# A decoder layer in split float32: first rounding on two engines, squares behind the up weights, a split bias product, and the last head's scores later

## The chip, the cores and the metric

One core of a Trainium2 chip. The metric is the device time of one execution in microseconds. The engines are named PE (TensorE), ACT (ScalarE), DVE (VectorE), POOL (GpSimd) and SP (SyncE, which here issues loads).

## The reference

The kernel computes one decoder layer for 256 tokens of width 1024, in float32: a half step of a SwiGLU feed-forward net, a mixer of two groups of attention heads that share a table of relative position biases, cross attention to 256 memory tokens in 4 heads of width 256, a second half step, and a final norm. Cut to what matters here:

```python
def rms_norm(x, g):
    xf = x.astype(jnp.float32)
    y = xf * lax.rsqrt(jnp.mean(xf * xf, axis=-1, keepdims=True) + NORM_EPS)
    return (y * g.astype(jnp.float32)).astype(x.dtype)

def swiglu(x, w_gu, w_down):
    gu = x @ w_gu
    g, u = jnp.split(gu, 2, axis=-1)
    return (jax.nn.silu(g) * u) @ w_down

def reference(x, mem, ...):
    x = x + 0.5 * swiglu(rms_norm(x, g_ffn1), w_ffn1_gu, w_ffn1_down)
    h = rms_norm(x, g_mix)           # q, k, v of both groups
    ...                              # s = q @ k.T * scale + rel_bias[bucket of the distance]
    x = x + concat([ya, yb]) @ w_out
    # cross attention, per head
    #   s = q @ k.T * 256 ** -0.5; p = softmax(s); o = p @ v
    x = x + o @ w_co
    x = x + 0.5 * swiglu(rms_norm(x, g_ffn2), w_ffn2_gu, w_ffn2_down)
    return rms_norm(x, g_final)
```

## The kernel before, in words

PE multiplies in a rounded 32-bit type, fp32r. To keep float32 accuracy an operand is split in a high part (rounded by a copy on ACT) and a low part (the difference, on DVE): `wsplit` (L124) does it for a weight chunk of 128x1024, with the copy at L125 and the difference at L126; `split` does it for activations (L320 and L321, or with a gain as scale L323 and L324). A product of two split operands is `mm3`, three products (L188 high by high, L189 low of the first by high, L190 high by low of the second), or `mm2`: one of 512 columns over the high and low part of the activations (L224, and L238 in the first stage where both halves are 256 wide), and one of 256 columns with the low part of the weight (L228).

Weights come from device memory in chunks through SP's queue (L118) into a few `raw` buffers and are split into a pool of `w` buffers, each of which is used again when PE has read it for the last time.

The order of the work on PE is the order in which the code issues it, helped by a small event list: `later(us, f, ...)` calls `f` when a clock has moved on by that many modelled microseconds; every product moves the clock by its modelled length (`tick`). The order on the other engines is set by a scheduler, except in `start`, which is in a manual schedule for all engines.

The pieces that the change touches:

- `start` (L754): loads the input x in pieces (`x0`), warms PE with WARM and then WARM - 1 products of the identity (L770, L796), turns x with transposes (L779), and computes the first gate chunk `pg0` over k = 0 to 7 with `mmT_wide` (L238), while `prepare` brings the next two k: the weight's split, copies of the turned x to X (L783), and their split with the gain (L323, L324). `token_squares` sums the squares of x (L337, ACT with accumulation): half at k = 2, half at k = 5 behind the split of the first "up" weights, where the sum is added (L806). From it come the mean, a power on POOL (L330), a diagonal on DVE (L376) and products that spread it over the rows (L382).
- `bias_table` and `bias_rows` (L88, L96): load the logarithm table `lnt`, the one-hot table `oht` of 32x383 and `rel_bias` as `rbt` (L93); 4 modelled us later multiply `rbt` and `oht` in full float32 (L98), add, and send the rows through device memory on POOL's queue. On SP's queue the load of `rbt` stands right behind the loads of the gains (L72) of `start`, and those of `lnt` (L91) and `oht` (L92) among later weight loads.
- `cross_qp` (L678): projects the query, splits it, and for head h sets off `scores(h)` after a delay: three products each (L188 to L190) for the halves, the maximum (L693), the exponential on ACT (L698), the division (L701); and `turn(h)` 5 modelled us after the scores, which transposes the probabilities (L709) and splits them (L320, L321).
- `cross_o(h)` (L729): waits until `PT[h]`, the turned probabilities, has been issued, and multiplies them with the values (L188 to L190); its output is split as well. The call of `addT(w_co, OT, ...)` that follows multiplies the outputs of the heads with `w_co`; `cross_o` of heads 2 and 3 is called between its blocks.

Of the kernel before, what the change touches and what calls it, by code (L numbers as in the profile page):

```python
# [9 lines left out]
F32 = mybir.dt.float32  # L10
F32R = mybir.dt.float32r
BF = mybir.dt.bfloat16
AF = mybir.ActivationFunctionType
OP = mybir.AluOpType
# [8 lines left out]
NB = 383  # L23
# [5 lines left out]
def layer_kernel(ctx, tc, x_in, mem_in, g_ffn1, w_gu1, w_dn1, g_mix, w_in, rel_bias, g_out_a, g_out_b,  # L29
# [57 lines left out]

    def bias_table():  # L88
        lnt = work.tile([16, NB], F32, tag="g1", name="lnt", bufs=3)
        oht = work.tile([32, NB], F32, tag="g1", name="oht", bufs=3)  # L90
        nc.sync.dma_start(lnt, lnc)  # L91
        nc.sync.dma_start(oht, onehot)  # L92
        nc.sync.dma_start(rbt, rel_bias)  # L93
        later(4.0, bias_rows, lnt, oht)

    def bias_rows(lnt, oht):  # L96
        ps = bank()
        nc.tensor.matmul(ps[:16, :NB], rbt, oht, start=True, stop=True)  # L98
        rb = work.tile([16, 384], F32, tag="u1", name="rb")
        nc.vector.tensor_add(rb[:, :NB], ps[:16, :NB], lnt)  # L100
        nc.vector.memset(rb[:, NB:], 0.0)
        scr = dram.tile([16, 32, 384], F32, name="scr")
        nc.gpsimd.dma_start(scr, rb.unsqueeze(1).broadcast_to([16, 32, 384]))
        for i in range(2):
            f = const.tile([P, 8, 256], F32, tag="big", name="F", bufs=2)
            for a in range(4):
                src = bass.AP(tensor=scr.tensor, offset=scr.offset + 127 - 32 * a + i * 8 * 32 * 384,
                              ap=[[383, 32], [32 * 384, 8], [1, 256]])
                later(5.0 * (i * 4 + a), nc.gpsimd.dma_start, f[32 * a:32 * a + 32], src)
            F.append(f)  # L110
# [12 lines left out]

    def wsplit(w, raw, a, b):  # L124
        nc.scalar.activation(w[:, 0, a:b], raw[:, a:b], AF.Copy)  # L125
        nc.vector.tensor_tensor(w[:, 1, a:b], raw[:, a:b], w[:, 0, a:b].bitcast(F32), OP.subtract)  # L126

    def cols(wd, k0, nk, c0, n):
# [29 lines left out]
    def later(delay, fn, *args):  # L158
        events.append((clock[0] + delay, len(events_seq), fn, args))
        events_seq.append(0)  # L160
        events.sort(key=lambda e: e[:2])
# [171 lines left out]
    def token_squares(src, ss):  # L333

        for tb in range(2):
            junk = work.tile([P, 512], BF, tag="sq", name="junk", bufs=3)
            nc.scalar.activation(junk, src[:, tb * 512:tb * 512 + 512], AF.Square, accum_out=ss[:, tb:tb + 1])  # L337
# [340 lines left out]
    def cross_qp(xs, K, st):  # L678
# [37 lines left out]
        for c in range(2):  # L716
            for blk, ps in enumerate(projT(colchunk(w_cq, c * 512, 512), xs, 4, spread=(c == 0), whole=4 * (c == 0))):
                if blk % 2 == 0:
                    Q.append(slot())
                if ps.shape[-1] == 512:  # L720
                    t = work.tile([P, 256], F32, tag="sq", name="hq", bufs=3)
                    halves(t, ps)
                    ps = t
                split(Q[-1], blk % 2, 1, ps)
                if blk % 2:
                    later(3.0 + 3.0 * (blk // 2) * (c == 0), scores, c * 2 + blk // 2)
        return PT

    def cross_o(V, PT, OT, h):  # L729
# [24 lines left out]
    def start():  # L754
# [18 lines left out]
        def prepare(j):  # L773
            banks = [bank(), bank()] if j == 0 else [bank()] * 2
            xp = [banks[i][:, i * 256:i * 256 + 256] for i in range(2)]
            for i in range(2):
                for tb in range(2):
                    o = tb * 512 + ((j * 2 + i) % 4) * P
                    nc.tensor.transpose(xp[i][:, tb * P:(tb + 1) * P], x0[j // 2][:, o:o + P], ident)  # L779
            if j > 0:  # L780
                wsplit(ws[j], raws[j], 0, 1024)
                for i in range(2):
                    nc.scalar.activation(X[j * 2 + i], xp[i], AF.Copy)  # L783
            for i in range(2):
                split(xs[j], i, 1, X[j * 2 + i] if j else xp[i], gain("ffn1", j * 2 + i))
                if j == 0:
                    wsplit(ws[j], raws[j], i * 512, i * 512 + 512)
            if j == 0:
                for i in range(2):
                    nc.scalar.activation(X[i], xp[i], AF.Copy)  # L790
# [1 line left out]
        xss = [small.tile([P, 2], F32, tag=f"xss{hf}", name="xss", bufs=1) for hf in range(2)]  # L792

        prepare(0)
        for i in range(WARM - 1):
            nc.tensor.matmul(gps[:, :P], ident, ident, start=True, stop=True)  # L796
        for k in range(KT):
            mmT_wide(pg0, first, xs, k, k == 0, k == KT - 1)
            if k % 2 == 0 and k < KT - 2:
                prepare(k // 2 + 1)  # L800
                if k == 2:
                    token_squares(x0[0], xss[0])
            if k == 5:
                up.extend(colchunk(w_gu1, FF, 512))
                token_squares(x0[1], xss[1])
                nc.vector.tensor_tensor(xss[0], xss[0], xss[1], OP.add)  # L806
                st.given(xss[0], 7.0)
                later(4.0, turn_gains)
# [162 lines left out]
```

## Time and profile before

| | us |
|---|---|
| median of three runs | 606.03 |
| the runs | 605.70, 606.03, 606.17 |
| the profiled execution | 605.48 |
| its span, first to last instruction | 603.7 |
| PE busy | 595.4 (99% of the span) |
| DVE busy | 435.5 (72%) |
| ACT busy | 348.2 (58%) |
| POOL busy | 51.9 (9%) |

The profiled execution's time is its span and 1.8 us around it. The granted clock of PE was 0.998 of full speed over the span. A product's record covers its way through the array, and records overlap, so what a product costs PE is read from start to start. In a timeline row the first number is the start, the second the length from the start of the first to the end of the last of the instructions that the row joins; in brackets stands how long the engine was idle before, and what ended that.

### The profile page before, as it was taken

To read this page: it belongs to the slowest core of one execution; us is meant where nothing else is said; L and a number is where in the kernel's file an instruction comes from. 1 tells how busy PE (TensorE), PEld (TensorE's weight loads), DVE (VectorE), ACT (ScalarE), POOL (GpSimd) and SP (SyncE) were. 2 spreads that over 40 slices of the span, in tenths; PEclk is the share of its full clock that TensorE was granted. 3 is DMA by queue.
4 is the path that set the end of the run, shared out by engine and by line. 5 is a ranking of instruction groups with operands and counts; after the bars stand their busy time and mean duration, and the time that the engine had idled before them with its cause. 6 is when DMAs were issued, how large, how long until landed. Compare 5 with 4: busy or idle time off the path is not lost.

```text
span 603.7 us, 9507 instructions
## 1 busy us (share of the span) xinstructions
PE 595.4 (99%) x3528; PEld 519.9 (86%) x3528; DVE 435.5 (72%) x730; ACT 348.2 (58%) x606; POOL 51.9 (9%) x83
## 2 busy tenths in 40 slices
PE   9999999999999999999999999999999999999995
PEld 8988888888899888888888899888888888888885
DVE  4878756897565876766897787869878787784424
ACT  6856445655545677656675565657754655653303
POOL 0000210000010102103300120003100000000000
PEclk9999999999999999999999999999999999999999
DMA  7866998577577636444446544444565566476401
GB/s 238 286 209 224 214 245 248 181 241 242 174 232 221 210 107 209 140 140 140 141 126 214 186 154 159 141 139 132 160 220 191 171 209 209 154 265 197 153 0 71
DMA packets 58990, 110.04 MB, mean 182 GB/s; under 512 B 3760, under 2 KB 14608, under 8 KB 58944
## 3 DMA queue, kind: packets, MB, share of 16 engines
q1 hardware_dynamic: 57664, 105.49, 54.7%
q0 software_dynamic: 832, 2.88, 2.7%
q10 hardware_dynamic: 448, 1.05, 0.5%
q8 instruction: 28, 0.46, 0.3%
q14 instruction: 18, 0.15, 0.1%
HBM read 107.58 MB, written 1.84 MB: 181 GB/s over the span
## 4 chain that ended last, share of the span: by engine, by line
PE 92%; DVE 3%; ACT 1%; issue 1%; DMA 1%; POOL 0%; POOLq 0%; ACTq 0%; SPq 0%
PE bank L224 42%; PE bank L228 21%; PE bank L188 7%; PE bank L189 7%; PE bank L190 7%; PE bank L238 3%; DVE w L126 1%; PE bank L518 1%; PE bank L575 1%; PE bank L558 1%; DMA raw<-in_w_co_dram 1%; DVE slot L321 1%; ACT w L125 1%; ACT cpt L698 0%; PE bank L770 0%
## 5 line engine op out<-in xcount | busy, mean ns | idle before, releaser
L224 PE MATMUL bank<-slot,w 128*128 128x512 f32 x1130 | 353.7, 396 | 0.0
L126 DVE TENSOR_TENSOR w<-raw,w 128x1024 fp32r<-128x1024 f32 (+1 forms) x197 | 237.1, 1217 | 82.5 <-ACT w L125 81.7
L125 ACT ACTIVATE w<-raw 128x1024 fp32r<-128x1024 f32 (+1 forms) x197 | 202.5, 1051 | 87.3 <-PE bank L190 43.4
L228 PEld LDWEIGHTS bank<-slot,w 128*128 128x128 f32 x1130 | 209.7, 188 | 48.6 <-issue 1.0
L228 PE MATMUL bank<-slot,w 128*128 128x256 f32 x1130 | 222.5, 279 | 0.0
L224 PEld LDWEIGHTS bank<-slot,w 128*128 128x128 f32 x1130 | 174.0, 189 | 2.5 <-issue 0.6
L188 PE MATMUL bank<-w,slot 128*128 128x512 f32 (+1 forms) x156 | 60.6, 389 | 0.0
L190 PE MATMUL bank<-w,slot 128*128 128x512 f32 (+1 forms) x156 | 60.0, 384 | 0.0
L189 PE MATMUL bank<-w,slot 128*128 128x512 f32 (+1 forms) x156 | 59.9, 384 | 0.0
L277 ACT ACTIVATE hv<-bank 128x256 f32<-128x256 f32 x108 | 39.7, 374 | 34.9 <-PE bank L228 34.4
L190 PEld LDWEIGHTS bank<-w,slot 128*128 128x128 f32 x156 | 29.3, 188 | 6.0
L188 PEld LDWEIGHTS bank<-w,slot 128*128 128x128 f32 x156 | 29.3, 188 | 5.8 <-issue 0.3
L189 PEld LDWEIGHTS bank<-w,slot 128*128 128x128 f32 x156 | 29.3, 188 | 5.5
L320 ACT ACTIVATE slot<-u 128x512 fp32r<-128x512 f32 x22 | 13.8, 629 | 33.7 <-DVE u L434 33.7
L238 PE MATMUL bank<-slot,w 128*128 128x256 f32 x240 | 31.8, 289 | 0.0
L238 PEld LDWEIGHTS bank<-slot,w 128*128 128x128 f32 x240 | 30.0, 194 | 0.5 <-DVE slot L324 0.4
L355 POOL TENSOR_TENSOR ssq<-ssq,sq 128x256 f32<-128x256 f32 x22 | 20.6, 935 | 78.5 <-ACT sq L350 78.3
L429 ACT ACTIVATE g<-g 128x512 f32<-128x512 f32 x22 | 13.8, 631 | 20.6 <-DVE g L292 20.6
L324 DVE SCALAR_TENSOR_TENSOR slot<-X,gT,slot 128x256 fp32r<-128x256 f32 x30 | 19.4, 658 | 6.9 <-ACT slot L323 6.9
L278 DVE TENSOR_TENSOR u<-bank,hv 128x256 f32<-128x256 f32 x40 | 16.7, 418 | 8.8 <-ACT hv L277 8.7
L278 DVE TENSOR_TENSOR g<-bank,hv 128x256 f32<-128x256 f32 x40 | 16.3, 417 | 8.3 <-ACT hv L277 8.3
L323 ACT ACTIVATE slot<-X,gT 128x256 fp32r<-128x256 f32 x30 | 14.8, 505 | 13.0 <-DVE X L303 12.9
(129 smaller groups left out, 494.0 us busy)
## 6 DMA issues: line engine op xcount, KB each, us to landing
raw<-in_w_ffn_gu_dram SPq DMA_DIRECT2D x88, 512.0 KB, 4.8
raw<-in_w_ffn_down_dram SPq DMA_DIRECT2D x44, 512.0 KB, 4.5
raw<-in_w_ckv_dram SPq DMA_DIRECT2D x16, 512.0 KB, 5.3
raw<-in_w_in_dram SPq DMA_DIRECT2D x12, 512.0 KB, 3.6
raw<-in_w_in_dram SPq DMA_DIRECT2D x24, 256.0 KB, 4.1
raw<-in_w_out_dram SPq DMA_DIRECT2D x8, 512.0 KB, 4.4
raw<-in_w_cq_dram SPq DMA_DIRECT2D x8, 512.0 KB, 5.8
raw<-in_w_co_dram SPq DMA_DIRECT2D x8, 512.0 KB, 4.0
```

What stands on the lines that cost most here:

```text
L125: nc.scalar.activation(w[:, 0, a:b], raw[:, a:b], AF.Copy)
L126: nc.vector.tensor_tensor(w[:, 1, a:b], raw[:, a:b], w[:, 0, a:b].bitcast(F32), OP.subtract)
L188: nc.tensor.matmul(ps, ah, bh, start=start, stop=False)
L189: nc.tensor.matmul(ps, al, bh, start=False, stop=False)
L190: nc.tensor.matmul(ps, ah, bl, start=False, stop=stop)
L224: nc.tensor.matmul(ps, w[:, 0, o + blk * P:o + (blk + 1) * P], both(xs, k), start=k == first, stop=False)
L228: nc.tensor.matmul(ps[:, :256], w[:, 1, o + blk * P:o + (blk + 1) * P], both(xs, k)[:, :256], start=False, stop=k == last)
L238: nc.tensor.matmul(ps, w[:, wp_, o + blk * P:o + (blk + 1) * P], a, start=start and i == 0, stop=stop and i == 2)
L277: nc.scalar.activation(t, ps[:, 256:], AF.Copy)
L278: nc.vector.tensor_tensor(out, ps[:, :256], t, OP.add)
L324: nc.vector.scalar_tensor_tensor(l, src, g, h.bitcast(F32), OP.mult, OP.subtract)
L355: (eng or nc.gpsimd).tensor_tensor(new, self.ss, sq, OP.add)
```

## The change

Four edits. In `start` the first half of the first weight is rounded by ACT and DVE, 256 columns each (`wsplit2`), and one product of the identity is left out behind `prepare(0)`. All four squares of x are issued at k = 5, behind the up weights. In `bias_table` the one-hot table gets a 384th column of zeros, `rbt` is split into `rbs` (ACT, DVE), the one-hot table is copied to fp32r (`ohr`, ACT), and `bias_rows` makes two fp32r products of 384 columns. In `cross_qp` the delay of the last head's scores is 5.7 instead of 3.0 modelled us (the others keep 3, 6 and 3).

```diff
@@ -87,15 +87,22 @@
 
     def bias_table():
         lnt = work.tile([16, NB], F32, tag="g1", name="lnt", bufs=3)
-        oht = work.tile([32, NB], F32, tag="g1", name="oht", bufs=3)
+        oht = work.tile([32, 384], F32, tag="g1", name="oht", bufs=3)
+        nc.vector.memset(oht[:, NB:], 0.0)
         nc.sync.dma_start(lnt, lnc)
-        nc.sync.dma_start(oht, onehot)
+        nc.sync.dma_start(oht[:, :NB], onehot)
         nc.sync.dma_start(rbt, rel_bias)
-        later(4.0, bias_rows, lnt, oht)
-
-    def bias_rows(lnt, oht):
+        rbs = small.tile([32, 2, 16], F32R, tag="rbs", name="rbs", bufs=1)
+        nc.scalar.activation(rbs[:, 0], rbt, AF.Copy)
+        nc.vector.tensor_tensor(rbs[:, 1], rbt, rbs[:, 0].bitcast(F32), OP.subtract)
+        ohr = work.tile([32, 384], F32R, tag="pt", name="ohr", bufs=4)
+        nc.scalar.activation(ohr, oht, AF.Copy)
+        later(4.0, bias_rows, lnt, ohr, rbs)
+
+    def bias_rows(lnt, ohr, rbs):
         ps = bank()
-        nc.tensor.matmul(ps[:16, :NB], rbt, oht, start=True, stop=True)
+        for i in range(2):
+            nc.tensor.matmul(ps[:16, :384], rbs[:, i], ohr, start=i == 0, stop=i == 1)
         rb = work.tile([16, 384], F32, tag="u1", name="rb")
         nc.vector.tensor_add(rb[:, :NB], ps[:16, :NB], lnt)
         nc.vector.memset(rb[:, NB:], 0.0)
@@ -123,6 +130,12 @@
 
     def wsplit(w, raw, a, b):
         nc.scalar.activation(w[:, 0, a:b], raw[:, a:b], AF.Copy)
+        nc.vector.tensor_tensor(w[:, 1, a:b], raw[:, a:b], w[:, 0, a:b].bitcast(F32), OP.subtract)
+
+    def wsplit2(w, raw, a, m, b):
+
+        nc.scalar.activation(w[:, 0, a:m], raw[:, a:m], AF.Copy)
+        nc.vector.tensor_copy(w[:, 0, m:b], raw[:, m:b])
         nc.vector.tensor_tensor(w[:, 1, a:b], raw[:, a:b], w[:, 0, a:b].bitcast(F32), OP.subtract)
 
     def cols(wd, k0, nk, c0, n):
@@ -723,7 +736,7 @@
                     ps = t
                 split(Q[-1], blk % 2, 1, ps)
                 if blk % 2:
-                    later(3.0 + 3.0 * (blk // 2) * (c == 0), scores, c * 2 + blk // 2)
+                    later(((3.0, 6.0), (3.0, 5.7))[c][blk // 2], scores, c * 2 + blk // 2)
         return PT
 
     def cross_o(V, PT, OT, h):
@@ -783,8 +796,10 @@
                     nc.scalar.activation(X[j * 2 + i], xp[i], AF.Copy)
             for i in range(2):
                 split(xs[j], i, 1, X[j * 2 + i] if j else xp[i], gain("ffn1", j * 2 + i))
-                if j == 0:
-                    wsplit(ws[j], raws[j], i * 512, i * 512 + 512)
+                if j == 0 and i == 0:
+                    wsplit2(ws[j], raws[j], 0, 256, 512)
+                elif j == 0:
+                    wsplit(ws[j], raws[j], 512, 1024)
             if j == 0:
                 for i in range(2):
                     nc.scalar.activation(X[i], xp[i], AF.Copy)
@@ -792,17 +807,16 @@
         xss = [small.tile([P, 2], F32, tag=f"xss{hf}", name="xss", bufs=1) for hf in range(2)]
 
         prepare(0)
-        for i in range(WARM - 1):
+        for i in range(WARM - 2):
             nc.tensor.matmul(gps[:, :P], ident, ident, start=True, stop=True)
         for k in range(KT):
             mmT_wide(pg0, first, xs, k, k == 0, k == KT - 1)
             if k % 2 == 0 and k < KT - 2:
                 prepare(k // 2 + 1)
-                if k == 2:
-                    token_squares(x0[0], xss[0])
             if k == 5:
                 up.extend(colchunk(w_gu1, FF, 512))
-                token_squares(x0[1], xss[1])
+                for hf in range(2):
+                    token_squares(x0[hf], xss[hf])
                 nc.vector.tensor_tensor(xss[0], xss[0], xss[1], OP.add)
                 st.given(xss[0], 7.0)
                 later(4.0, turn_gains)
```

The order of the instructions, as built, moves in three places (line numbers of the code behind its 14 new lines are higher by 7 to 15: L125 is L132, L126 L133, L188 L201, L224 L237, L228 L241, L320 L333, L321 L334, L323 L336, L337 L350, L698 L711, L709 L722, L783 L796).

ACT in the first stage, behind the third weight's rounding, up to the squares at k = 5. Before:

```order
L783 ACTIVATE X_92<-bank 128x256
L783 ACTIVATE X_93<-bank 128x256
L323 ACTIVATE slot<-X_92,gT_82 128x256
L323 ACTIVATE slot<-X_93,gT_82 128x256
L337 ACTIVATE junk,xss<-slot 128x512 x2
L125 ACTIVATE w<-raw 128x1024
L783 ACTIVATE X_94<-bank 128x256
L783 ACTIVATE X_95<-bank 128x256
L323 ACTIVATE slot<-X_94,gT_82 128x256
L323 ACTIVATE slot<-X_95,gT_82 128x256
L125 ACTIVATE w<-raw 128x1024 x4
L337 ACTIVATE junk,xss<-slot 128x512 x2
```
Now:

```order
L96 ACTIVATE rbs<-rbt 32x16
L796 ACTIVATE X_92<-bank 128x256
L796 ACTIVATE X_93<-bank 128x256
L336 ACTIVATE slot<-X_92,gT_82 128x256
L336 ACTIVATE slot<-X_93,gT_82 128x256
L132 ACTIVATE w<-raw 128x1024
L796 ACTIVATE X_94<-bank 128x256
L796 ACTIVATE X_95<-bank 128x256
L336 ACTIVATE slot<-X_94,gT_82 128x256
L336 ACTIVATE slot<-X_95,gT_82 128x256
L132 ACTIVATE w<-raw 128x1024 x4
L350 ACTIVATE junk,xss<-slot 128x512 x4
```
The two squares between the third stage's scaled copies (L323) and the fourth weight (L125) have gone to the others behind the up weights; the copy of `rbt` to `rbs` (L96) stands in front of the copies of X_92.

ACT in cross attention, from the split of the outputs of head 1 to that of head 3. Here cpt is a half of the probabilities, w a weight, and slot_4337 (before) and slot_4358 (now) are the turned probabilities of the last head, slot_4343 and slot_4342 the output of head 2, slot_4367 and slot_4374 that of head 3. Before:

```order
L320 ACTIVATE slot_4267<-bank_4208 128x2x256
L698 ACTIVATE cpt_4242,cl_4243<-bank_4229,cnm_4240,c16_4236 128x256
L698 ACTIVATE cpt_4261,cl_4262<-bank_4248,cnm_4259,c16_4255 128x256
L125 ACTIVATE w_4575<-raw_4573 128x1024
L320 ACTIVATE slot_4337<-bank_4332 128x2x256
L320 ACTIVATE slot_4343<-bank_4322 128x2x256
L125 ACTIVATE w_4580<-raw_4578 128x1024
L320 ACTIVATE slot_4367<-bank_4354 128x2x256
```
Now:

```order
L333 ACTIVATE slot_4236<-bank_4215 128x2x256
L132 ACTIVATE w_4582<-raw_4580 128x1024
L711 ACTIVATE cpt_4295,cl_4296<-bank_4282,cnm_4293,c16_4289 128x256
L711 ACTIVATE cpt_4314,cl_4315<-bank_4301,cnm_4312,c16_4308 128x256
L333 ACTIVATE slot_4342<-bank_4329 128x2x256
L132 ACTIVATE w_4587<-raw_4585 128x1024
L333 ACTIVATE slot_4358<-bank_4353 128x2x256
L333 ACTIVATE slot_4374<-bank_4361 128x2x256
```
A weight now stands before the exponentials, and one (w_4587) between the split of head 2's output and that of the last head's probabilities, with the split of head 3's output right behind. On DVE the low parts stand in the same order: that of w_4587 between those of slot_4342 and slot_4358.

PE in cross attention, from the transposes of the last head's probabilities to the first products of `cross_o` of that head. Before:

```order
L709 MATMUL bank_4332<-ident_83,cpt_4242 128x128
L709 MATMUL bank_4332<-ident_83,cpt_4261 128x128
L709 MATMUL bank_4332<-ident_83,cpt_4242 128x128
L709 MATMUL bank_4332<-ident_83,cpt_4261 128x128
L188 MATMUL bank_4322<-slot_4217,slot_3541 128x256
L189 MATMUL bank_4322<-slot_4217,slot_3541 128x256
L190 MATMUL bank_4322<-slot_4217,slot_3541 128x256
L224 MATMUL bank_4296<-slot_4267,w_4281 128x512 x2
L228 MATMUL bank_4296<-slot_4267,w_4281 128x256 x2
L224 MATMUL bank_4297<-slot_4267,w_4281 128x512 x2
L228 MATMUL bank_4297<-slot_4267,w_4281 128x256 x2
L188 MATMUL bank_4354<-slot_4337,slot_3502 128x256
```
Now, from the last blocks of `w_co` before the transposes:

```order
L237 MATMUL bank_4265<-slot_4236,w_4250 128x512 x2
L241 MATMUL bank_4265<-slot_4236,w_4250 128x256 x2
L237 MATMUL bank_4266<-slot_4236,w_4250 128x512 x2
L241 MATMUL bank_4266<-slot_4236,w_4250 128x256 x2
L722 MATMUL bank_4353<-ident_83,cpt_4295 128x128
L722 MATMUL bank_4353<-ident_83,cpt_4314 128x128
L722 MATMUL bank_4353<-ident_83,cpt_4295 128x128
L722 MATMUL bank_4353<-ident_83,cpt_4314 128x128
L201 MATMUL bank_4361<-slot_4358,slot_3509 128x256
L202 MATMUL bank_4361<-slot_4358,slot_3509 128x256
L203 MATMUL bank_4361<-slot_4358,slot_3509 128x256
```
What stood between the transposes and the products that read their split is gone: the transposes come right before them. At the other end the last head's scores, before directly behind cross_o of head 1, have moved behind 15 of the 16 products of the first four blocks of `w_co` (w_4245, bank_4263 to bank_4266), which now stand there; w_4250 is the next weight of `w_co`, and its last use is the row before the transposes.

## Rows read from the trace of the kernel before

**Rows 1.** The page: busy time by engine; the chain that ended last, by engine.
```profile
PE 595.4 (99%) x3528; PEld 519.9 (86%) x3528; DVE 435.5 (72%) x730; ACT 348.2 (58%) x606; POOL 51.9 (9%) x83
...
PE 92%; DVE 3%; ACT 1%; issue 1%; DMA 1%; POOL 0%; POOLq 0%; ACTq 0%; SPq 0%
```

**Rows 2.** Timeline, PE, first stage (start us, us, what).
```profile
16.80 1.88 PE L238 MATMUL bank<-slot,w 128*128 128x256 f32 x11
...
22.72 1.48 PE L238 MATMUL bank<-slot,w 128*128 128x256 f32 x11
```

**Rows 3.** Timeline, PE, around the bias product.
```profile
59.35 0.39 PE L224 MATMUL bank<-slot,w 128*128 128x512 f32 x1
...
59.67 0.81 PE L98 MATMUL bank<-oht,rbt 32*16 32x383 f32 x2
...
60.42 0.50 PE L224 MATMUL bank<-slot,w 128*128 128x512 f32 x1
```

**Rows 4.** Timeline, PE, cross attention.
```profile
383.35 0.28 PE L188 MATMUL bank<-slot 128*128 128x256 f32 x1
...
383.59 0.28 PE L190 MATMUL bank<-slot 128*128 128x256 f32 x1
383.99 0.38 PE L188 MATMUL bank<-slot 128*128 128x256 f32 x1
384.93 0.39 PE L189 MATMUL bank<-slot 128*128 128x256 f32 x1 [0.55 <-DVE slot L321]
385.15 0.28 PE L190 MATMUL bank<-slot 128*128 128x256 f32 x1
...
386.68 0.62 PE L224 MATMUL bank<-slot,w 128*128 128x512 f32 x2
...
387.38 0.63 PE L224 MATMUL bank<-slot,w 128*128 128x512 f32 x2
...
391.25 0.60 PE L709 MATMUL bank<-ident,cpt 128*128 128x128 f32 x4
```

**Rows 5.** Timeline, ACT, cross attention.
```profile
382.55 1.09 ACT L125 ACTIVATE w<-raw 128x1024 fp32r<-128x1024 f32 x1
383.49 0.44 ACT L320 ACTIVATE slot<-hq 128x256 fp32r<-128x256 f32 x1
...
391.88 1.09 ACT L320 ACTIVATE slot<-bank 128x512 fp32r<-128x512 f32 x2 [1.85 <-PE bank L709]
393.63 1.06 ACT L125 ACTIVATE w<-raw 128x1024 fp32r<-128x1024 f32 x1 [0.66 <-PE bank L228]
```

**Rows 6.** Groups by line, PE, 2 to 9 us (xcount | busy, mean ns).
```profile
L796 PE MATMUL bank<-ident 128*128 128x128 f32 x8 | 1.9, 421 | 0.0
```

**Rows 7.** Timeline, SP's queue, ACT and DVE, first stage.
```profile
10.96 0.32 SPq L93 DMA_DIRECT2D rbt<-in_rel_bias_dram  x1
...
12.72 0.66 ACT L783 ACTIVATE X<-bank 128x256 f32<-128x256 f32 x2 [0.70 <-PE bank L779]
...
13.81 0.88 DVE L324 SCALAR_TENSOR_TENSOR slot<-X,gT,slot 128x256 fp32r<-128x256 f32 x2 [0.53 <-ACT slot L323]
14.07 0.63 ACT L337 ACTIVATE junk<-slot 128x512 bf16<-128x512 f32 x1
...
15.29 1.05 ACT L125 ACTIVATE w<-raw 128x1024 fp32r<-128x1024 f32 x1
```

**Rows 8.** The tile rbt: its transfer, from issue to landing.
```profile
DMA to landing us min/median/max: 2.6/2.6/2.6
```

**Rows 9.** Timeline, DVE and PE's loads, end of the first stage.
```profile
23.74 0.16 DVE L806 TENSOR_TENSOR xss<-xss 128x2 f32<-128x2 f32 x1
...
25.60 0.53 PEld L382 LDWEIGHTS bank<-dg,ones 128*128 128x128 f32 x4
```

**Rows 10.** Timeline, DVE, cross attention.
```profile
382.72 0.69 DVE L321 TENSOR_TENSOR slot<-bank,slot 128x512 fp32r<-128x512 f32 x1
383.32 1.22 DVE L126 TENSOR_TENSOR w<-raw,w 128x1024 fp32r<-128x1024 f32 x1
```

## The prediction

> **What bounds the kernel now.** I read the page's busy shares and its chain first, then the waits and the timeline of the three places that the change touches. TensorE is busy for 99% of the span and carries 92% of the chain that ended last [rows 1]. So an edit is worth what it does to the starts of PE's products: PE loses time only where its next product waits, or where it computes something longer than needed. Three such places lie near the edits.
>
> In the first stage 11 products of 256 columns take 1.88 us from 16.80, where 11 of the same kind take 1.48 us from 22.72 [rows 2]: 0.40 us are lost, to roundings that ScalarE (ACT) and VectorE (DVE) bring late. At 59.67 two instructions of the fp32 bias product stand between two L224 products [rows 3]. And at the last head's scores PE runs 383.35, then every 0.12 us to 383.59, and then waits: the next three start at 383.99, 384.93 and 385.15 [rows 4], since ACT delivers the rounded query at 383.49 + 0.44 [rows 5] and DVE its low part after that. Instead of 0.36 they take 1.56 us: **1.20 us are lost**. The last of these rows also shows that after a real wait the next gap is 0.22 instead of 0.12, so I add 0.1 to each new wait.
>
> The sums below are made against the profiled execution, 605.48 us; the median of the three runs, 606.03, lies 0.55 above it, and I carry that over unchanged.
>
> **First edit: rounding on two engines, one dummy product less.** Four dummy products are eight instructions of 1.9 us together [rows 6], so one less is 0.47 of PE, and halving the ACT part of the first rounding (DVE casts the other half beside it) is there to let PE use that. But the products of k = 2 wait for the low part of the next weight, whose transfer ACT awaits; what is gained earlier is waited for there. I take 0; bounds -0.47 and 0.
>
> **Squares later and the new rbs on ACT.** The order shows two things in the first stage. The two squares, ACT 14.07 to 15.29 [rows 7], go behind the eighth weight: 1.22 us of ACT are free there. But `rbs` from `rbt` is put on ACT between the third rounding and the copies of X_92, and ACT works in order. `rbt` is issued at 10.96 [rows 7] and lands 2.6 us later [rows 8], at 13.53; nobody needed it in before until 59.67. ACT would be at its place at about 12.0, and began the X_92 copies at 12.72 [rows 7], after PE's transposes. Now it waits until 13.53, spends about 0.2 on the tiny copy (an estimate from the 0.16 of the small DVE operation at 23.74 [rows 9] and a little more), and X_92 starts at about 13.64, 0.91 later. SP issues nothing that waits for `rbs`. Behind it are the two scaled roundings and DVE's low parts, 13.81 in before [rows 7], now 14.72. PE had no slack there: it reached the products of k = 4 at about 13.84 with no gap, just behind their high part, which ended before DVE's 13.81. So it now waits 0.88 + 0.1 = **+0.98**.
>
> From there the squares that are gone pay back: the next weight's rounding, 15.29 [rows 7], would come at 14.98 even with the delay, and the late low parts that cost 0.40 from 16.80 [rows 2] are then in time for a PE that is itself 0.98 later: **-0.40**. At the other end four squares of 0.61 each stand behind the eighth weight instead of two; the sum of squares moves from 23.74 [rows 9] by about 1.02. Behind it are the mean, POOL's power, DVE's diagonal and PE's L382 at 25.60 [rows 9]. PE arrives there 0.58 later, and waits some 0.1, plus 0.1: **+0.2**. Sum of the start **+0.75** (rounded down by 0.03). Bounds: +0.4, if PE absorbs part of the wait on products of the half before, to +1.0, if the 0.40 doesn't vanish wholly.
>
> By the page "DMA: Bandwidth & Descriptors" of the Trainium skill, section "Latency and other measured facts", a tiny transfer needs at least about 0.8 us, and reading device memory takes longer the more it is loaded. The landing of 2.6 us in this trace is far above that floor, under loaded queues, and is the one that I use. By the floor `rbt` would land at 11.76 and there would be no wait, and the sum would be that of rival B, below.
>
> **Bias product.** From 59.67 to the next L224 at 60.42 [rows 3] PE is given to L98: 0.75, and the neighbours' extra gaps make it some 0.85. No row has an fp32r product of 384 columns; between 0.12 for 256 [rows 4] and 0.23 for 512 (0.70 of a block of two 512 and two 256, [rows 4]) it is 0.175 by columns, so two take 0.35: **-0.5**. Bounds: 0 (32-row weights and the change of kind cost as much again) and -0.59 (the longer value with no extra gap). The new ACT and DVE operations lie beside PE, at 49 us and before, where ACT is under two thirds busy. Two loads change places on SP; nobody waits for them on PE.
>
> **Scores of the last head.** Removed: **-1.20**. In place of the scores the first four blocks of the output projection now follow at 383.35. They need the first head's low part, DVE 382.72 + 0.69 = 383.41 [rows 10], so PE starts at about 383.46 and the next gap is longer: **+0.2**. Up to the last head's transposes PE then has 8 blocks of 0.70 (386.68 to 387.38, [rows 4]) and 24 products of 0.12 for the scores and cross_o of head 2: 5.58 + 2.88 = 8.46, so the transposes start at about 392.06, and the last of the four, 0.11 apart, at 392.39. The probabilities are ready by some 391, although ACT takes a weight before them; no wait there.
>
> Now comes what the order shows. In before, seven rows of work stood on PE between the transposes at 391.25 [rows 4] and the cross_o of head 3, and their split, ACT from 391.88 [rows 5], was hidden. In the change **nothing** stands between them, and on ACT and DVE a weight (w_4587) is rounded first. That rounding waits for PE's last use of an older weight, as the one at 393.63 did [rows 5], so I let it start 0.2 after the block's end, 392.26. The next ACT operation comes 0.94 later (382.55 to 383.49, [rows 5]): the high part of the last head's probabilities runs 393.21 to 393.81, half of the 1.09 of the pair [rows 5], and PE begins cross_o at 393.87 instead of 392.50. On DVE the weight's low part starts when ACT's rounding ends, 393.32, and takes about 1.13 till the next (383.32, 1.22 long, [rows 10]); then the probabilities' low part, 0.69 [rows 10], ends at 395.18. The third product of cross_o needs it: 395.24 instead of 392.74, with 0.1 for the restart **+2.6**. So the place gives -1.20 + 0.2 + 2.6 = **+1.6**. Lower bound: if nothing stood before the split, its high part would run from 392.70, the low part to 394.02, and the third product come at 394.08: a wait of 1.34 + 0.1, the place +0.4. Upper bound: +2.0, a weight that lands late by 0.4. After it, the last head's output is needed only four blocks later, as in before.
>
> **Sum:** 0 + 0.75 - 0.5 + 1.6 = +1.9 (+1.87): 607.4 against 605.48, and **607.9** against the median.
>
> **Rivals.**
>
> *B, `rbt` is there in time.* The transfer of 2 KB lands by about 12.0, under light load on the queues, and the copy costs ACT only its 0.2. Against it: nothing before it on SP changes, so the 2.6 us of [rows 8] should repeat. The start gives +0.1 - 0.40 + 0.2 = -0.1, the sum +1.0: 607.0. It decides where `rbt` lands before PE's transposes end, at about 12.4.
>
> *C, not slower: the split of the last head's probabilities isn't held up by the weight.* Place: ACT's rows behind the last exponentials. If w_4587 finds its buffer free before the transposes (its older weight read by PE earlier than I take it), it is rounded before 392.3, and the wait on PE is only the bare chain of 1.44. The place then gives +0.4 and the sum +0.65: 606.7, which a measurement of this kernel can't tell from no change (about 0.2%, 1.2 us). Against it: the like rounding at 393.63 did wait for PE [rows 5]. With B as well the sum is -0.2: 605.8. To be faster by over 1.2 us, the whole wait of 2.6 would have to be away, and the bare chain alone leaves 1.44 of it.
>
> *D, the clock.* No wait of before is longer than 0.94 on PE in this stage, and the granted clock stayed full; a wait of 1.1 and then 1.1 is new. At half the clock the rest of cross_o, 12 products of 0.12, would take 1.4 more and two blocks behind it as much again: 609.3 to 610.7. The Trainium skill, page "TensorE: Matmul & The Clock Gate", section "HAM oscillation — how this bites in real kernels", tells of waits between groups of products that bring the clock to its lower level; no row here has a wait of this kind, so it has a small chance only.
>
> **How the numbers follow.** The forecast has 0.64 (its own bounds +1.2 to +2.7, 607.2 to 608.7), B 0.15, C 0.12, B and C together 0.03, D 0.04, others 0.02. The range 606.5 to 608.8 holds the forecast, B and C, and leaves out about one in ten to 0.15. Faster (below 604.8) needs what none of the cases gives, 0.05. Same (604.8 to 607.2) takes B, C, both, and the lowest part of the forecast's own range: 0.30. Slower: 0.65.
>
> **What would show it.** Right: in the timeline after, ACT's L96 starts at about 13.5 behind an idle stretch that ends with the transfer of `rbt`; PE has a gap of about 1 us near 14; no gap near 17 to 18; L105 takes about 0.35 at the bias; no gap at the scores; and two gaps of about 1.3 and 1.1 us in front of the first and third product of the last cross_o, released by ACT L333 and DVE L334. Wrong: a last cross_o that starts with no gap, or a gap of under 1.5 us in all; a granted clock below full around it; or a bias product as long as before.

## The result, and the profile after

The changed kernel takes **609.85 us** (median of six runs, 609.30 to 610.32), the kernel before 605.93 (six runs, 605.15 to 606.32): a ratio of 1.0065, 95% interval 1.0054 to 1.0076. It is slower by 3.9 us. The forecast was slower, 607.9 with a range of 606.5 to 608.8: the right side, and outside the range.

PE is busy for 98% of the span instead of 99%, with two instructions less and 4.1 us more of span (607.8 against 603.7 [rows 1]). The page of the changed kernel, busy times:

```profile
PE 597.0 (98%) x3526; PEld 521.1 (86%) x3526; DVE 436.4 (72%) x733; ACT 348.8 (57%) x608; POOL 51.8 (9%) x83
```

Of the 4.1 us, 1.6 count as busy (597.0 against 595.4): PE didn't only wait, it also worked longer on nearly the same products. The timeline shows where.

**First stage.** The timeline of the changed kernel (start us, us, what, idle before and its end), which answers to [rows 7]:

```profile
10.99 0.32 SPq L94 DMA_DIRECT2D rbt<-in_rel_bias_dram  x1
...
13.37 0.22 ACT L96 ACTIVATE rbs<-rbt 32x16 fp32r<-32x16 f32 x1 [1.31 <-DMA rbt<-in_rel_bias_dram]
13.49 0.62 ACT L796 ACTIVATE X<-bank 128x256 f32<-128x256 f32 x2
...
14.56 1.74 PE L251 MATMUL bank<-slot,w 128*128 128x256 f32 x12 [0.42 <-ACT slot L336]
...
16.13 0.60 PE L792 MATMUL bank<-ident,slot 128*128 128x128 f32 x4
...
22.54 0.26 PE L76 MATMUL bank<-ident,grow 48*128 48x48 f32 x1
```

ACT stands idle for 1.31 us until `rbt` lands, X_92 starts 0.77 later than in the kernel before (13.49 against 12.72 [rows 7]), and PE waits for what follows. The transfer took 2.4 us; [rows 8] had 2.6. The end of the stage, which answers to [rows 9]:

```profile
21.76 1.06 ACT L132 ACTIVATE w<-raw 128x1024 fp32r<-128x1024 f32 x1 [0.70 <-DMA raw<-in_w_ffn_gu_dram]
...
24.57 0.61 ACT L350 ACTIVATE junk<-slot 128x512 bf16<-128x512 f32 x1
...
25.31 0.16 DVE L820 TENSOR_TENSOR xss<-xss 128x2 f32<-128x2 f32 x1 [1.23 <-ACT junk L350]
...
26.94 0.68 PE L395 MATMUL bank<-dg,ones 128*128 128x128 f32 x4 [0.71 <-DVE dg L389]
```

The same places in the kernel before, ACT's timeline, then PE's:

```profile
21.42 1.06 ACT L125 ACTIVATE w<-raw 128x1024 fp32r<-128x1024 f32 x1 [0.90 <-DMA raw<-in_w_ffn_gu_dram]
...
15.40 0.60 PE L779 MATMUL bank<-ident,slot 128*128 128x128 f32 x4
...
22.19 0.26 PE L76 MATMUL bank<-ident,grow 48*128 48x48 f32 x1
...
25.72 0.61 PE L382 MATMUL bank<-dg,ones 128*128 128x128 f32 x4
```

The four squares start only after the eighth weight, whose transfer ACT awaits in both kernels, and the sum comes at 25.31 instead of 23.74: 1.57 later, where 1.02 was forecast. PE waits for the diagonal (`dg`), which is built from that sum, and reaches its products at 26.94 instead of 25.72.

**Bias product.** PE's timeline, which answers to [rows 3]:

```profile
60.65 0.39 PE L237 MATMUL bank<-slot,w 128*128 128x512 f32 x1
...
60.97 0.52 PE L105 MATMUL bank<-ohr,rbs 32*16 32x384 f32 x2
...
61.42 0.50 PE L237 MATMUL bank<-slot,w 128*128 128x512 f32 x1
```

From 60.65 to 61.42 are 0.77 us, against 1.07 from 59.35 to 60.42: -0.30. The bias product starts 1.30 later than before, and behind it PE is 1.00 late.

**Last head.** PE's timeline, which answers to [rows 4]:

```profile
384.42 0.73 PE L237 MATMUL bank<-slot,w 128*128 128x512 f32 x2
...
392.97 0.60 PE L722 MATMUL bank<-ident,cpt 128*128 128x128 f32 x4
394.76 0.39 PE L201 MATMUL bank<-slot 128*128 128x256 f32 x1 [1.19 <-ACT slot L333]
...
396.14 0.38 PE L203 MATMUL bank<-slot 128*128 128x256 f32 x1 [0.87 <-DVE slot L334]
396.36 0.28 PE L201 MATMUL bank<-slot 128*128 128x256 f32 x1
...
397.60 0.41 PE L203 MATMUL bank<-slot 128*128 128x256 f32 x1
397.82 1.05 PE L237 MATMUL bank<-slot,w 128*128 128x512 f32 x2
...
399.10 1.05 PE L237 MATMUL bank<-slot,w 128*128 128x512 f32 x2
...
400.37 0.62 PE L237 MATMUL bank<-slot,w 128*128 128x512 f32 x2
```

The same products in the kernel before, PE's timeline from the fourth product of the last cross_o on:

```profile
393.79 0.28 PE L188 MATMUL bank<-slot 128*128 128x256 f32 x1
...
394.87 0.63 PE L224 MATMUL bank<-slot,w 128*128 128x512 f32 x2
...
396.27 0.63 PE L224 MATMUL bank<-slot,w 128*128 128x512 f32 x2
```

No wait at the scores, and two waits before the first and the third product of the last cross_o, as forecast. What releases them, in the timeline of ACT, then of DVE:

```profile
393.17 1.06 ACT L132 ACTIVATE w<-raw 128x1024 fp32r<-128x1024 f32 x1 [0.80 <-PE bank L241]
394.13 0.58 ACT L333 ACTIVATE slot<-bank 128x512 fp32r<-128x512 f32 x1
...
394.26 1.23 DVE L133 TENSOR_TENSOR w<-raw,w 128x1024 fp32r<-128x1024 f32 x1 [1.16 <-ACT w L132]
395.40 0.68 DVE L334 TENSOR_TENSOR slot<-bank,slot 128x512 fp32r<-128x512 f32 x1
```

The weight waits for PE and stands before the probabilities on both engines: 394.13 is 0.92 later than the forecast's 393.21, and 395.40 is 0.91 later than its 394.49 (its end, 395.18, less 0.69): PE's transposes come at 392.97, 0.91 later than the forecast's 392.06. But from 396.9 on a 256-column product takes 0.215 from start to start, and a block takes 1.28 (397.82 to 399.10) where [rows 4] have 0.70. The same trace by stretches (us, busy of PE, PEld, DVE, ACT, POOL with counts, PEclk, DMA share, GB/s):

```profile
394.00:396.80 2.80, 1.17 (x7) 0.96 (x8) 1.83 (x2) 0.71 (x2) 0.00 (x0) 1.00 0.16 50
396.80:398.00 1.20, 1.20 (x8) 1.20 (x7) 0.00 (x0) 0.00 (x0) 0.00 (x0) 0.55 0.83 266
398.00:400.20 2.20, 2.20 (x9) 1.81 (x8) 0.69 (x1) 0.60 (x1) 0.00 (x0) 0.50 0.22 83
400.20:403.00 2.80, 2.80 (x17) 2.44 (x17) 0.00 (x0) 1.03 (x2) 0.00 (x0) 0.98 0.00 0
```

PE's granted clock is 0.50, its lower level, from about 396.9 to 400.2. It fell 0.7 us after the second wait had ended, and PE was busy all the while until it rose again. This was rival D. All six runs show a mean clock of 0.994 or 0.995, where the kernel before has 0.996 to 0.999.

The whole difference, read at the same products in both traces:

| step | forecast, us | traces, us | read at |
|---|---|---|---|
| start | +0.75 | +1.30 | bias product, 59.67 and 60.97 |
| bias product | -0.5 | -0.30 | 1.07 and 0.77 |
| scores and the waits of the last cross_o | +1.6 | +1.57 | its fourth product, 393.79 and 396.36, less 1.00 |
| lower clock | 0 (rival D) | +1.53 | 396.27 and 400.37, less 2.57 |
| sum | +1.87 | +4.10 | spans 603.7 and 607.8 |

The forecast's three terms as rounded add up to +1.85. The start's term is taken from one pair of traces; up to PE's transposes at 12.10 (12.09 before) the two agree, so it belongs to what comes behind them. The lower clock cost the rest of cross_o 0.38 (396.36 to 397.82 against 393.79 to 394.87) and the two blocks behind it 1.15 (397.82 to 400.37 against 394.87 to 396.27).

### The profile page after: what moved, and what is told of

The parts are those of the page before. It is cut to its first block, busy times and chain, and to the rows that moved or that the text cites. A ratio compares the mean times of both kernels' runs of the same rounds, so it can differ in the third digit from the quotient of the medians.

```text
span 607.8 us, 9507 instructions
## 1 busy us (share of the span) xinstructions
PE 597.0 (98%) x3526; PEld 521.1 (86%) x3526; DVE 436.4 (72%) x733; ACT 348.8 (57%) x608; POOL 51.8 (9%) x83
## 4 chain that ended last, share of the span: by engine, by line
PE 93%; DMA 3%; issue 1%; ACT 1%; DVE 1%; SPq 1%; POOL 0%; POOLq 0%
PE bank L237 43%; PE bank L241 22%; PE bank L201 7%; PE bank L203 7%; PE bank L202 7%; DMA raw<-in_w_ffn_gu_dram 3%; PE bank L251 2%; PE bank L531 1%; PE bank L588 1%; PE bank L571 1%; PE bank L395 0%; DVE w L133 0%; ACT w L132 0%; ACT junk L350 0%; SPq L765 0%
## 5 line engine op out<-in xcount | busy, mean ns | idle before, releaser
L237 PE MATMUL bank<-slot,w 128*128 128x512 f32 x1130 | 354.6, 397 | 0.0
L133 DVE TENSOR_TENSOR w<-raw,w 128x1024 fp32r<-128x1024 f32 (+1 forms) x196 | 236.6, 1222 | 81.5 <-ACT w L132 80.0
L132 ACT ACTIVATE w<-raw 128x1024 fp32r<-128x1024 f32 (+1 forms) x196 | 201.8, 1053 | 90.1 <-PE bank L203 43.8
L241 PEld LDWEIGHTS bank<-slot,w 128*128 128x128 f32 x1130 | 210.3, 188 | 48.8 <-issue 1.0
L241 PE MATMUL bank<-slot,w 128*128 128x256 f32 x1130 | 223.1, 280 | 0.0
L237 PEld LDWEIGHTS bank<-slot,w 128*128 128x128 f32 x1130 | 174.5, 189 | 2.3 <-issue 0.3
L201 PE MATMUL bank<-w,slot 128*128 128x512 f32 (+1 forms) x156 | 60.6, 389 | 0.0
L201 PEld LDWEIGHTS bank<-w,slot 128*128 128x128 f32 x156 | 29.3, 188 | 5.8 <-issue 0.3
L333 ACT ACTIVATE slot<-u 128x512 fp32r<-128x512 f32 x22 | 13.8, 630 | 32.5 <-DVE u L447 32.5
L337 DVE SCALAR_TENSOR_TENSOR slot<-X,gT,slot 128x256 fp32r<-128x256 f32 x30 | 19.5, 659 | 7.9 <-ACT slot L336 7.9
L336 ACT ACTIVATE slot<-X,gT 128x256 fp32r<-128x256 f32 x30 | 14.8, 504 | 13.0 <-DVE X L316 13.0
```

What stands on the lines that cost most here:

```text
L201: nc.tensor.matmul(ps, ah, bh, start=start, stop=False)
L237: nc.tensor.matmul(ps, w[:, 0, o + blk * P:o + (blk + 1) * P], both(xs, k), start=k == first, stop=False)
L241: nc.tensor.matmul(ps[:, :256], w[:, 1, o + blk * P:o + (blk + 1) * P], both(xs, k)[:, :256], start=False, stop=k == last)
L337: nc.vector.scalar_tensor_tensor(l, src, g, h.bitcast(F32), OP.mult, OP.subtract)
```

## The experiments

Twelve kernels were run, each against the kernel before on the same chip: runs 1 to 4 on one, 5 to 8 on a second, 9 to 12 on a third. A mean granted clock of 0.995 or less counts as "clock fell"; the runs of the kernel before have 0.996 or more. Where it fell is seen only in the traces of the change and of run 1, in both at the last cross_o.

**1. The last head's delay alone**, in the kernel before:

```diff
-                    later(3.0 + 3.0 * (blk // 2) * (c == 0), scores, c * 2 + blk // 2)
+                    later(((3.0, 6.0), (3.0, 5.7))[c][blk // 2], scores, c * 2 + blk // 2)
```

> The kernel before with only the last head's delay changed to 5.7. Theory: the place alone costs what the trace of the change shows there, about 1.5 us of waits (1.3 and 1.1 us before the last cross_o, less the 1.2 us saved at the scores, with restarts) and about 1.7 us of products at half the clock behind them; +3.1 in all, 609.0. The granted clock falls after the second wait. Rival 1, only the waits belong to this place and the clock fell because of the rest of the change: +1.5, 607.4. Rival 2, the waits come only because the start had shifted the rest: no change, 605.9.

Measured: 608.39 us against 605.85, ratio 1.0045 (1.0030 to 1.0060). The six runs fall in two groups: three with a mean clock of 0.994 or 0.995 take 608.58 to 609.79, three with 0.997 or 0.998 take 607.08 to 608.20. The kept trace, of an execution with the clock fallen, has the same two waits, 1.19 and 0.87 us idle, with the start of the kernel before: they belong to this edit, and the change's start has no part in them. That trace's 609.62 holds some 1.1 us that aren't the edit's: its first weight landed later, and the bias product stands at 60.79 instead of 59.67. The clock fell in half of the executions only, so each of rival 1 and the theory describes one of the two groups; that it varies was expected by neither.

**2. The change without that delay** (the line above put back in the changed kernel).

> The changed kernel with the delay of the last head's scores back at 3.0. Theory: left are the start, +1.3 by the traces up to the bias product, and the bias product, -0.3; +1.0, 606.9, with a granted clock as in the kernel before. Rival: the start costs nothing in the end, because what is late there is caught up later, 605.6 or less.

Measured: 606.59 against 605.85, ratio 1.0012 (1.0003 to 1.0021); no run of eleven with the clock fallen. The time is 0.3 less than expected, and 0.7 of the start and the bias product together remains, where the traces have 1.0: the rival falls.

**3. The waits filled.** Products of the identity, whose result nobody reads, stand in both waits:

```diff
         op = bank()
+        fb = bank() if h == 3 else None
+        fill = lambda n: [nc.tensor.matmul(fb[:, :P], ident, ident, start=True, stop=True) for _ in range(n * (h == 3))]
+        fill(5)
...
+                    nc.tensor.matmul(o, va, ph, start=True, stop=False)
+                    nc.tensor.matmul(o, vb, ph, start=False, stop=False)
+                    fill(4)
+                    nc.tensor.matmul(o, va, pl, start=False, stop=False)
...
```

> The changed kernel with 5 products of the identity in the first and 4 in the second wait before the last cross_o, into a bank of their own; they are shorter together than the waits. Theory: the waits stay as long, but PE does not stand idle and the clock stays at its upper level: 1.7 us less than the change, 608.2. Rival 1, something else than the idle time lowers the clock: as the change, 609.9, with the clock falling in the same place. Rival 2, the fills delay the products they stand before: 610.4 or more.

Measured: 608.03, ratio 1.0039 (1.0027 to 1.0051); no run of five with the clock fallen. PE's timeline:

```profile
392.65 0.60 PE L722 MATMUL bank<-ident,cpt 128*128 128x128 f32 x4
393.09 1.28 PE L746 MATMUL bank<-ident 128*128 128x128 f32 x10
394.45 0.39 PE L755 MATMUL bank<-slot 128*128 128x256 f32 x1
...
394.80 1.06 PE L746 MATMUL bank<-ident 128*128 128x128 f32 x8
395.83 0.39 PE L758 MATMUL bank<-slot 128*128 128x256 f32 x1
...
397.11 0.63 PE L237 MATMUL bank<-slot,w 128*128 128x512 f32 x2
...
397.81 0.62 PE L237 MATMUL bank<-slot,w 128*128 128x512 f32 x2
```

From the transposes to the first real product are 1.80 us, against 1.79 in the changed kernel (392.97 to 394.76), and from the first real product to the third 1.38, as there (394.76 to 396.14): the waits are as long, and useless work in them makes the kernel 1.8 us faster (1.7 with each against its own runs of the kernel before). The blocks behind run at 0.70. So it is PE standing idle in these waits that lowers the clock here, not what the engines around it do.

**9 and 10. One wait filled**, the other left.

> The changed kernel with the 5 products of the identity in the first wait of the last cross_o alone; the second wait, some 0.9 us idle, stays. Theory: the clock falls only where both waits follow each other closely, so it stays up here in every run: 608.1, granted clock as in the kernel before. Rival, the second wait alone is enough: some or all runs at 609.8 with a mean clock near 0.995.

> The changed kernel with the 4 products of the identity in the second wait alone; the first, 1.2 us idle, stays. Theory: as with the first wait filled, the clock stays up: 608.1. Rival, the first wait alone is enough: some or all runs at 609.8 with a mean clock near 0.995.

Measured: 608.26 (1.0038, 1.0025 to 1.0050) and 607.90 (1.0035, 1.0022 to 1.0049) against 605.59; the clock fell in none of five and none of five runs. With one wait open it fell in none of ten executions, with both open (the change, runs 1 and 4) in 12 of 17. Both together lower it, and neither did alone, as far as five executions each can show. Why it fell in some executions and not in others stays open: the kept trace of run 4, below, has both waits as long as the change and the clock up.

**6. Cover for the split.** In the changed kernel, cross_o of the last head is issued two blocks later:

```diff
-                               lambda: cross_o(V, PT, OT, 3), (4, every), (6, every)))
+                               (4, (0, 1)), lambda: cross_o(V, PT, OT, 3), (4, (2, 3)), (6, every)))
```

> The changed kernel with cross_o of the last head issued two blocks of the output projection later, behind blocks 0 and 1 of k = 4 and 5, so that products stand between the transposes and it. Theory: the two waits shrink from 1.2 and 0.9 us idle to about 0.5 each, a wait of some 0.2 comes elsewhere, and the clock stays up: 1.0 less wait and 1.7 less slow products, 607.2, with a granted clock like the kernel before. Rival, the clock falls for shorter waits too: 608.8.

Measured: 606.86, ratio 1.0016 (1.0007 to 1.0026), no run of eleven with the clock fallen. PE's timeline at the same two products as above:

```profile
395.96 0.39 PE L201 MATMUL bank<-slot 128*128 128x256 f32 x1 [0.22 <-ACT slot L333]
...
396.69 0.39 PE L203 MATMUL bank<-slot 128*128 128x256 f32 x1 [0.22 <-DVE slot L334]
```

Idle 0.22 twice instead of 1.19 and 0.87. So the missing cover, which the order of the instructions showed, made the waits.

**4. No wait for `rbt`.** In the changed kernel rbs is made on DVE, with a zero column of `ohr` added, so that it can't stand before the one-hot table's copy:

```diff
-        nc.scalar.activation(rbs[:, 0], rbt, AF.Copy)
-        nc.vector.tensor_tensor(rbs[:, 1], rbt, rbs[:, 0].bitcast(F32), OP.subtract)
         ohr = work.tile([32, 384], F32R, tag="pt", name="ohr", bufs=4)
         nc.scalar.activation(ohr, oht, AF.Copy)
+        nc.vector.tensor_scalar(rbs[:, 0], rbt, ohr[:, 383:384].bitcast(F32), None, OP.add)
+        nc.vector.tensor_tensor(rbs[:, 1], rbt, rbs[:, 0].bitcast(F32), OP.subtract)
```

> The changed kernel with rbs computed on DVE behind the copy of the one-hot table (the sum of rbt and a zero of that copy, so that it cannot stand early), so ACT waits for no transfer of rbt. Theory: PE's wait near 14 us goes, but the wait before the products with the diagonal (26.94) is set by four squares behind an up weight whose transfer is awaited, and takes over most of it: about 0.35 us less than the change, 609.5. Rival, both waits belong to rbs: about 1.0 less, 608.85.

Measured: 609.07, ratio 1.0048 (1.0035 to 1.0061). The median mixes three runs with the clock fallen (609.07 to 609.53) and two without (607.65 and 607.84), so it can't decide between 0.35 and 1.0. The trace, of an execution without, can. ACT's timeline, then PE's:

```profile
12.69 0.66 ACT L796 ACTIVATE X<-bank 128x256 f32<-128x256 f32 x2 [0.68 <-PE bank L792]
...
26.59 0.68 PE L395 MATMUL bank<-dg,ones 128*128 128x128 f32 x4 [1.12 <-DVE dg L389]
...
394.53 0.39 PE L201 MATMUL bank<-slot 128*128 128x256 f32 x1 [1.19 <-ACT slot L333]
...
395.90 0.38 PE L203 MATMUL bank<-slot 128*128 128x256 f32 x1 [0.87 <-DVE slot L334]
396.12 0.28 PE L201 MATMUL bank<-slot 128*128 128x256 f32 x1
...
398.59 0.63 PE L237 MATMUL bank<-slot,w 128*128 128x512 f32 x2
```

X_92 starts as in the kernel before, PE's wait near 14 us is gone, and the wait for the diagonal grows from 0.71 to 1.12: PE has 26.59 instead of 26.94, 0.35 less. At the last head the waits are those of the change to the hundredth, but the clock stays up: from the fourth product of cross_o to the third block are 2.47 us (396.12 to 398.59), against 4.01 in the change (396.36 to 400.37). That is the price of the clock once more, 1.54, between two kernels with the same waits.

**5. The squares alone**, in the kernel before: both calls of `token_squares` at k = 5.

> The kernel before with only the squares moved behind the up weights. Theory: the four squares end near 24.9 and PE waits for the diagonal at 26.6 instead of 25.7, whatever was saved at 17 to 18 us: +0.9, 606.75. Rival, the 0.4 saved there is what remains and the diagonal is in time: 605.45.

Measured: 606.80 against 605.89, ratio 1.0011 (1.0002 to 1.0019). DVE's sum and PE's wait in its timeline:

```profile
24.90 0.16 DVE L805 TENSOR_TENSOR xss<-xss 128x2 f32<-128x2 f32 x1 [1.22 <-ACT junk L337]
...
26.54 0.68 PE L382 MATMUL bank<-dg,ones 128*128 128x128 f32 x4 [1.27 <-DVE dg L376]
```

PE is at the diagonal at 26.54, in the kernel before at 25.72, right behind the load of [rows 9], and there is no `rbs` here at all. So of the start's 1.2 us at that point the squares cost 0.8 by themselves (0.9 by the runs' medians), and the wait for `rbt` only the rest.

**11. The first edit alone**, in the kernel before.

> The kernel before with the first edit alone (first half of the first weight rounded on two engines, one product of the identity less). Theory: PE's first products come up to 0.2 us earlier and wait that much longer at 11 us: no change, 605.9. Rival, the gain is kept: 605.45.

Measured: 605.65 against 605.59, ratio 1.0001 (0.9992 to 1.0010): no change, though the interval reaches down to the rival's gain. In the trace the first products of `pg0` start at 6.32 us instead of 6.46, but PE's transposes near 12 us start at 12.22 instead of 12.09: nothing of the gain is left there. In the changed kernel's own trace the two are 6.34 and 12.10.

**12. The split bias product alone**, with rbs as in run 4.

> The kernel before with the split bias product alone, rbs made behind the copy of the one-hot table. Theory: two fp32r products cost 0.29 us less from the product before them to the one behind: 605.6. Rival, half a microsecond as first taken: 605.4. Rival, the new copies late in ACT's queue cost it again: 605.9.

Inconclusive: 606.38 against 605.59, but with runs from 604.89 to 607.34; the ratio, estimated from all runs, is 1.0004 with an interval of 0.9993 to 1.0015, which holds -0.3 us as well as none. In its trace the two products take what they take in the change (59.74 to the next product at 60.20: 0.46, against 0.45 there).

**7. A version that keeps the gains**: the changed kernel with the squares back in their places, rbs as in run 4, cross_o as in run 6, and the last head's scores at 4.5 instead of 5.7.

> A version meant to keep the gains: squares as before, rbs behind the one-hot copy, last head's scores at 4.5 and cross_o of it two blocks later. Theory: bias product -0.3, the 1.2 us at the scores away with 0.2 to 0.4 of new waits: -1.2, 604.65. Rival, a new wait of over 1 us at the last cross_o again: 605.6 or more.

Measured: **604.61** against 605.89, ratio 0.9981 (0.9972 to 0.9989): faster than both kernels, by 1.3 us against the one before. PE's timeline at the last cross_o:

```profile
391.37 0.60 PE L722 MATMUL bank<-ident,cpt 128*128 128x128 f32 x4
391.72 0.48 PE L241 MATMUL bank<-slot,w 128*128 128x256 f32 x2
...
393.44 0.28 PE L201 MATMUL bank<-slot 128*128 128x256 f32 x1
393.56 0.28 PE L202 MATMUL bank<-slot 128*128 128x256 f32 x1
```

Between the transposes and the cross_o stand 1.72 us of other products (391.72 to 393.44), and it starts without a gap.

**8. The first two squares in a third place**, behind the last turned columns (k = 4), the rest as in run 7.

> As the version with the squares as before, but the first two squares stand behind the last two turned columns (k = 4), in front of the fifth weight, where ACT later waits 0.9 us for a transfer anyway. Theory: the 0.4 lost at 17 to 18 us is saved too, and the diagonal is only 0.2 late: 0.2 less than the version with the squares as before, 604.45. Rival, the weights behind them come late for PE or the diagonal does: 0.3 more than that version.

Measured: 605.12, ratio 0.9988 (0.9979 to 0.9997), 0.5 above run 7, though the two intervals overlap: not better, as the rival had it. Its trace shows PE waiting 0.18 us for the low part of a weight at 21.06, which the squares have pushed back; it also waits at the first weight, before the squares, so how much of the 0.5 is theirs stays open.

## Why the prediction was wrong, point by point

**The step that failed is rival D.** "No wait of before is longer than 0.94 on PE in this stage, and the granted clock stayed full", and from that "it has a small chance only", 0.04. That no row showed such a wait was taken for evidence that it does nothing; it was only the lack of evidence. The two waits had been worked out, 2.6 us with three products among them, and the clock fell behind them in every run of the change: +1.53 us, put at nothing in the forecast. The price that the rival gave was 1.4 for the rest of cross_o and as much again for two blocks behind it; measured were 0.38 and 1.15, since the clock fell only when four products of cross_o were left. That the whole time, 609.85, lies in the rival's 609.3 to 610.7 is in part luck: 0.70 of it is what the other terms were too low by.

The page "TensorE: Matmul & The Clock Gate" of the Trainium skill, section "HAM oscillation — how this bites in real kernels", tells of waits for transfers between groups of products, behind which the clock is at its lower level. The traces agree in direction, with a clock of 0.50 behind the two waits and 1.00 with either filled, but each wait of the page's example is longer than the two here together.

Without the clock the traces give +2.57, 608.5 against the median, inside the range and inside the forecast's own bounds; runs 3, 9 and 10, whose clock stayed up, show 607.9 to 608.3.

**The start was mis-sized**: +0.75 forecast, +1.30 measured. Its first wait was right in kind and too long: 0.98 forecast, where PE's transposes come at 16.13 instead of 15.40, 0.73 later; `rbt` landed some 0.15 sooner than taken. The -0.40 was right (0.35 of lateness remains at 22.54 against 22.19). The wait for the diagonal was put at 0.2 and is 0.87. The forecast moved the sum of squares by 1.02; it moved by 1.57. The two added squares count in full, 1.22, since right before the squares ACT waits for a weight's transfer in both kernels (0.90 us before, 0.70 now), so that the time freed earlier buys nothing; and that weight is rounded 0.34 later (21.76 against 21.42). PE, for its part, is 0.35 late there and not 0.58. In runs 4 and 5 PE's wait there is 1.12 and 1.27. The two terms were added as if each were there by itself; run 4 shows that they are in series, and that the first, taken away, comes back in the second to about half.

**The bias product** was put at -0.5 and gave -0.30. By columns a product would have taken 0.175; with 32 rows and 16 columns of weights the two take 0.45 to the next product, 0.22 each. The extra gap of the neighbours, counted as saved too, stayed: from the product before to the first of the two are 0.32 us in both kernels.

**The last head** came out within 0.03 us (+1.57 against +1.6), with idle times of 1.19 and 0.87 us for the two waits that were announced as 1.3 and 1.1 (from start to start, so that they hold the slow restart too), and the releasers as named. The working has slips of up to 0.15 us on the way (383.46 + 8.46 is not 392.06, 393.32 + 1.13 + 0.69 is not 395.18, and 13.53 with the copy's 0.2 is not 13.64); none of them makes the miss. Rival C fell: the weight did wait for PE (0.80 at 393.17). Run 6 confirms from the other side that cover was what lacked.

**The first edit** gave nothing that the runs can show, as forecast (run 11). **Rival B** fell by the 1.31 us that ACT waited.

## What to carry to other kernels

When a change moves a producer's work away from its place, look at what then stands between it and its consumer on every engine of the chain; here two engines' roundings in the wrong order cost twice what the moved wait had cost. On a matrix engine that hardly ever stood idle before, price a new wait with the clock included, above all two waits close together, and cover them with other products. And a delay that is taken out ahead of another one is worth only what the second does not take back.

## What was not expected of the hardware

Two waits of 1.19 and 0.87 us idle, two products apart, brought the granted clock to its lower level in 12 of 17 executions of three kernels, while one of them alone did so in none of ten (five with the first filled, five with the second). The same two waits, to the hundredth, left the clock up in the kept execution of run 4. Nine products of the identity into an unused bank, which add work and shorten no wait, made the kernel 1.8 us faster.
